# One addition per finished block moves from VectorE to GpSimd, and one pass gets another place in the order list

## The chip, the cores and the metric

The kernel runs on one core of one Trainium2 chip. Its time is the device time of one execution in microseconds (us). Beside it stands one profiled execution, taken by the hardware profiler, whose rows are quoted below: PE is TensorE, DVE is VectorE, ACT is ScalarE, POOL is GpSimd, SP is SyncE, whose only work here is to issue DMA transfers. L1323 is line 1323 of the kernel.

## The reference

One layer mixes 128 context tokens and 2048 latent tokens. Half of the channels go through a recurrence over tokens with a 64 x 64 state for each of 8 heads, once forward and once backward, and the two outputs are added, normalised for each head, gated and sent through an output projection:

```python
def step(S, inp):
    r_t, w_t, k_t, v_t, kk_t, a_t = inp
    s_kk = jnp.einsum('bdhij,bdhj->bdhi', S, kk_t)
    S = (S * w_t[..., None, :] - s_kk[..., :, None] * (kk_t * a_t)[..., None, :]
         + v_t[..., :, None] * k_t[..., None, :])
    return S, jnp.einsum('bdhij,bdhj->bdhi', S, r_t)
...
y = ys[:, 0] + jnp.flip(ys[:, 1], axis=1)
mean = jnp.mean(y, axis=-1, keepdims=True)
var = jnp.mean(jnp.square(y - mean), axis=-1, keepdims=True)
y = ((y - mean) * lax.rsqrt(var + GN_EPS)).reshape(b, t, A_WIDTH)
y = y * lp['gn_w'].astype(f32) + lp['gn_b'].astype(f32)
y = y + (bonus[..., None] * vh).reshape(b, t, A_WIDTH)
...
ya = ya.astype(x.dtype) * jax.nn.silu(g_a)
```

The kernel writes the last three lines as (normalised y) x gn_w x gate + q, where q holds gn_b and the bonus, already multiplied by the gate.

## The kernel before, in words

There are three phases. The first computes all projections and writes what the recurrence needs to HBM. The second is the scan, and the change lies there. The third is the output projection with the last normalisation.

**Stages and bodies of the scan.** The tokens are cut into chunks of 64. A stage handles 8 chunks of one pair of heads in each direction; there are 17 stages. The words of the list `SEQ` are the steps of one body of a software pipeline: `S00+0` is a step for the body's own stage, `zr+2` one for the stage two further on, `L0+4` a load for the stage four further on. Bodies -3 to -1 fill the pipeline, bodies 0 to 12 (up to `FIXED`) are the repeated ones, and after them a second list, `LATE`, gives every step with its stage and mixes in the third phase.

**What sets the order.** From body 0 on, PE, DVE and ACT execute exactly in the order of these lists. POOL and SP don't: their instructions are put in an order by a scheduler that estimates when each is ready. Every engine's queue, SP's too, is served strictly in order.

**The inverse, on POOL.** A chunk needs the inverse of a triangular 64 x 64 matrix. Its diagonal blocks of 32 rows come from step `I`, lines 1091 and 1094: for one stage 15 products (`ztmp`, m = 0 to 14) with two subtractions (`zt`) each, 45 instructions. The step `pre` (L1081, L1082, DVE) comes ahead of it and writes the `ab` that it reads; step `zr` (L1102, DVE) transposes the finished `zt`, after which `U` (L1119, PE) multiplies. In body b, `pre` works for stage b+3 and `zr` for stage b+2, so each inverse lies between the `pre` of one body and the `zr` of the next.

**The end of a block.** Where both directions of a block of 512 tokens are done, seven steps finish it, one block in each body: `fw` fetches the gate `sg` and squares y into `w` (L1298, ACT); `fr` sums the squares; `fq` takes the root (L1303, ACT); `fm` normalises y (L1306, DVE) and fetches q into the one buffer `w`; `T` transposes y into PSUM (L1317, PE); `fy` multiplies by gn_w and the gate (L1321, DVE, from PSUM into `sg`); `fa` adds q (L1323) and issues the store to `mixT` (L1327). `sg` and `w` have one buffer each: the next block's gate is fetched after the store has landed (L1286), and the next squares are written after the addition has read q. There are 17 such ends, 16 of latent blocks and one of the context.

Of the kernel before, what the change touches and what calls it, by code (L numbers as in the profile page):

```python
# [10 lines left out]
ALU = mybir.AluOpType  # L11
# [745 lines left out]
E111 sv71+-1 Ev111 E010 E101 y11+-1 E011 gsL1+2 fsL1+1 bu+1 Ev010 I+2 S20 Ev101 fw Ev011 sv20 S01 E100  # L757
fsL0+1 gsL0+2 sv01 fr Ev100 Gm1+3 Ge1+3 dg1+3 W+1 S11 Qm1+3 gh11+1 gh00+1 ab+3 fq Fm0+3 S30 n+1 Qe1+3 Qm0+3
L0+4 sv11 Fa0+3 Qe0+3 zi+3 sv30 S40 Fe0+3 fm S21 sv40 sv21 Fm1+3 L1+4 X0+1 S50 pre+3 T sv50 Fa1+3 Fe1+3 S31
S60 sv31 Xc00+1 init+1 y00 Xc10+1 X1+1 S41 Xc01+1 sv60 S70 svL0+2 zr+2 sv41 E000+1 sv70 fy Xc11+1 Ev000+1  # L760
zd+2 S51 gh01+2 U+2 y01 Gm0+4 E001+1 c0+2
"""
IN_PM = "E001 E011 E101 E110 Fm1 Gm1 Qm0 Qm1 X1".split()
# [1 line left out]
FIXED = 13  # L765
# [50 lines left out]
def phase2(K):  # L816
    nc, tc, A, S = K.nc, K.tc, K.A, K.S
    V, G, P, T = nc.vector, nc.gpsimd, nc.scalar, nc.tensor
# [99 lines left out]
    def tl(shape, tag, b, pool=None, dt=F32):  # L918
        return (pool or O.l0).tile(shape, dt, tag=tag, name=f"{tag}_{K.u()}", bufs=b)
# [73 lines left out]
    def psum(name, s, shape):  # L993

        pool, tag = pool_of(name, s)
        return pool.tile(shape, F32, tag=tag, name=f"ps{name}_{s}_{K.u()}")
# [253 lines left out]
    def outputs(name, s, st, gi):  # L1250

        g = st.g[gi]
        k = int(name[1])
        u = unit(g, 4 * k + 3)
        m = u % 2 if g.blk is None else u // 4
        ps = g.sp.pop(k)
        p, blk = g.units[0][0], g.blk
        y, there = ynew.setdefault((p, blk), (None, []))
        if y is None:
            y = tl([128, 4, 128], "y", 5)  # L1260
            ynew[p, blk] = y, there
        r = slice(m * 64, m * 64 + 64)
        src = ps[64:128].rearrange("p q h v -> p q (h v)")
        if m in there:
            V.tensor_tensor(y[r], src, y[r], ALU.add)
        else:
            P.copy(y[r], src)
        there.append(m)
        if len(there) == 4:
            ynew.pop((p, blk))  # L1270
            ends[s, gi] = finish(p, blk, y)
            pend.append((s, gi))

    def finish(p, blk, y):

        t0 = NCTX + 512 * blk if blk is not None else 0
        if blk is None:
            parts = [(pp_, slice(pp_ * 128, pp_ * 128 + 128)) for pp_ in range(4)]
        else:
            parts = [(p, slice(0, 512))]  # L1280

        def fetch(nm, t_):
            if blk is None:
                D(t_[:].rearrange("p (g t) -> p g t", t=128), S[nm][:, 0:128].rearrange("(g p) t -> p g t", p=128))
            else:
                D(t_[:], S[nm][p * 128:(p + 1) * 128, t0:t0 + 512])  # L1286

        heads = lambda x: x.rearrange("p q (h v) -> p (q h) v", h=2)
        per_head = lambda x: x[:].unsqueeze(2).broadcast_to((128, 8, 64))
        if blk is None:  # L1290
            mn = tl([128, 8], "ymn", 1)
            V.tensor_reduce(mn[:], heads(y[:]), mybir.AxisListType.X, ALU.add)
            V.scalar_tensor_tensor(heads(y[:]), per_head(mn), -1.0 / 64, heads(y[:]), ALU.mult, ALU.add)
            yield
        sg = tl([128, 512], "sg", 1)
        fetch("sg", sg)
        w = tl([128, 4, 128], "w", 1)
        P.activation(w[:], y[:], AF.Square)  # L1298
        yield
        ss = tl([128, 8], "yss", 2)  # L1300
        V.tensor_reduce(ss[:], heads(w[:]), mybir.AxisListType.X, ALU.add)
        yield
        P.activation(ss[:], ss[:], AF.Sqrt, bias=B.geps[:], scale=1.0 / 64)  # L1303
        yield
        V.reciprocal(ss[:], ss[:])
        V.tensor_tensor(heads(y[:]), heads(y[:]), per_head(ss), ALU.mult)  # L1306
        q = tl([128, 512], "w", 1)
        fetch("q", q)
        yield
        pt = psum("T", 0, [128, 512])  # L1310
        idm = B.idt[:]
        for i in range(4):
            if blk is None:
                dst = pt[:, i * 128:i * 128 + 128]
            else:
                dst = pt[:].rearrange("p (m q t) -> p m q t", m=2, q=4)[:, :, i]
            T.transpose(dst, y[:, i], idm if blk is None else idm.rearrange("p (m t) -> p m t", m=2))  # L1317
        yield
        o = sg
        for g_, cs in parts:  # L1320
            V.scalar_tensor_tensor(o[:, cs], pt[:, cs], B.gwh[:, g_:g_ + 1], sg[:, cs], ALU.mult, ALU.mult)  # L1321
        yield
        V.tensor_tensor(o[:], o[:], q[:], ALU.add)  # L1323
        if blk is None:
            D(S["mixT"][0:512, 0:128].rearrange("(g p) t -> p g t", p=128), o[:].rearrange("p (g t) -> p g t", t=128))
        else:
            D(S["mixT"][p * 128:(p + 1) * 128, t0:t0 + 512], o[:])  # L1327
        K.mixed[blk] = K.mixed.get(blk, 0) + 1
# [4 lines left out]
    def ending(name, s, st, gi):  # L1333
# [3 lines left out]
        if st.fin is not None:  # L1337
# [3 lines left out]
              zr=zrows, zd=zrows, c0=zcopies, c1=zcopies, U=merge, bu=merge, W=merge, n=merge, gh=gcopies, X=solve, Xc=solve,  # L1341
# [307 lines left out]
```

## Time and profile before

| what | us |
|---|---|
| median of three runs (1577.63 to 1589.78) | 1579.01 |
| the profiled execution's own time | 1579.98 |
| its span, first to last instruction | 1578.2 |
| PE busy, of the span | 1496.3 |
| DVE busy | 1138.5 |
| ACT busy | 772.6 |
| POOL busy | 574.6 |
| the 17 inverses on POOL, busy (L1094 217.6 + L1091 138.2) | 355.8 |

The page divides the span into 40 slices of 39.5 us and gives the busy tenths of each engine in each. A group's row gives a line, its engine and operation, the tile it writes and those it reads, its count, and then the busy time, the mean duration in ns and the idle time just before, with what ended it. A row of the timeline gives a start in us from the span's start and a duration. The chain of waits follows the work that ended last back from the end. The repeated bodies that finish a block lie between about 1036 and 1282 us.

### The profile page before, as it was taken

The numbers are of one execution on the slowest core, as the hardware profiler recorded it, in microseconds if no ns is written. First come the engines' busy times: TensorE is split into PE (matmuls) and PEld (weight loads), VectorE is DVE, ScalarE is ACT, GpSimd is POOL, SyncE is SP. The second block draws the span as 40 slices with busy tenths as digits, with TensorE's granted clock in tenths as the row PEclk, the third lists the DMA queues.
The fourth block names the chain that finished last, engine by engine and source line by source line (L and its number), as shares of the span: only waits on it lengthen the run. The fifth ranks groups of instructions, "written<-read, shape, count | busy, mean of one in ns | idle before, by whom it ended". The sixth has DMA issues, their size and how long they took to land.

```text
span 1578.2 us, 39386 instructions
## 1 busy us (share of the span) xinstructions
PE 1496.3 (95%) x16208; PEld 1377.9 (87%) x16208; DVE 1138.5 (72%) x1957; ACT 772.6 (49%) x1462; POOL 574.6 (36%) x962
## 2 busy tenths in 40 slices
PE   5899989999999999999999998999999997799998
PEld 2899989999999999899999997887888786678786
DVE  5999995673999735449995437899898987646533
ACT  4566652432555313225651107887878777523222
POOL 0133320000333100013322805888888887212221
PEclk9999999999999999999999998999999999999999
DMA  9669998663877875447887536566675754645442
GB/s 370 211 186 264 265 266 324 214 217 118 214 228 228 200 241 182 142 140 205 257 252 267 196 124 170 163 185 174 192 202 163 192 157 149 183 139 189 149 143 93
DMA packets 204580, 313.78 MB, mean 199 GB/s; under 512 B 58089, under 2 KB 147561, under 8 KB 190321
## 3 DMA queue, kind: packets, MB, share of 16 engines
q1 hardware_dynamic: 168816, 311.13, 63.6%
q10 hardware_dynamic: 35584, 0.14, 1.4%
q8 instruction: 127, 2.08, 0.6%
q14 instruction: 53, 0.43, 0.1%
HBM read 208.05 MB, written 103.17 MB: 197 GB/s over the span
## 4 chain that ended last, share of the span: by engine, by line
PE 61%; DVE 18%; DMA 8%; issue 5%; POOL 4%; ACT 3%; SPq 1%; ACTq 0%; DVEq 0%; POOLq 0%
PE psu L1503 4%; PE psu L1504 4%; PE psu L1505 4%; PE psE L1189 3%; POOL zt L1094 3%; PE mmb L182 2%; PE mmb L184 2%; PE mmb L183 2%; PE psS L1220 2%; PE mmc L182 2%; PE mmc L184 2%; PE mmc L183 2%; PE mmu L184 2%; PE mmgb L184 2%; PE mmu L182 2%
## 5 line engine op out<-in xcount | busy, mean ns | idle before, releaser
L1094 POOL TENSOR_TENSOR zt<-zt,ztmp 128x30 f32<-128x30 f32 (+7 forms) x510 | 217.6, 427 | 39.8
L1091 POOL TENSOR_TENSOR ztmp<-ab,zt 128x60 f32<-128x60 f32 (+7 forms) x255 | 138.2, 542 | 63.7 <-DVE ab L1082 44.0
L410 POOL TENSOR_TENSOR sh<-rawl 128x384 f32<-128x384 f32 (+1 forms) x48 | 46.9, 994 | 209.9 <-ACT rawl L401 209.9
L1220 PEld LDWEIGHTS psS<-sv,E 128*64 128x64 f32 x2176 | 81.3, 138 | 40.3 <-DVE sv L1246 18.8
L1220 PE MATMUL psS<-sv,E 128*64 128x64 f32 x2176 | 102.2, 229 | 14.8 <-DVE sv L1246 11.0
L1194 DVE TENSOR_TENSOR E<-psE,msk 128x512 f32<-128x512 f32 x136 | 90.6, 683 | 16.6 <-PE psE L1189 15.4
L1568 POOL TENSOR_TENSOR z<-z,x 128x512 f32<-128x512 f32 x32 | 42.7, 1338 | 146.5 <-DVE z L1562 86.0
L1175 ACT ACTIVATE stf<-psX 64x512 f32<-64x512 f32 x136 | 80.3, 591 | 11.2 <-PE psX L1171 8.8
L434 POOL TENSOR_TENSOR hsl<-sq,hsh 128x384 fp32r<-128x384 f32 (+1 forms) x24 | 34.0, 1417 | 130.6 <-ACT hsh L429 130.6
L1246 DVE TENSOR_TENSOR sv<-psS,pc 64x128 f32<-64x128 f32 x254 | 62.7, 273 | 22.5 <-PE psS L1220 21.8
L182 PE MATMUL mmg<-h,w 128*128 128x384 f32 (+1 forms) x216 | 70.8, 328 | 0.0
L183 PE MATMUL mmg<-h,w 128*128 128x384 f32 (+1 forms) x216 | 70.7, 327 | 0.0
L184 PE MATMUL mmg<-h,w 128*128 128x384 f32 (+1 forms) x216 | 70.6, 327 | 0.0
L219 POOL TENSOR_TENSOR hslq<-ssq,hshq 128x384 fp32r<-128x384 f32 (+1 forms) x4 | 4.8, 1208 | 176.9 <-ACT hshq L218 176.9
L182 PE MATMUL mmb<-h,w 128*128 128x384 f32 (+1 forms) x192 | 63.6, 331 | 5.8 <-DMA w<-scr_wsp 3.3
L184 PE MATMUL mmc<-h,w 128*128 128x384 f32 (+1 forms) x192 | 63.5, 331 | 0.9 <-DVE w L154 0.9
L182 PE MATMUL mmv<-h,w 128*128 128x384 f32 (+1 forms) x192 | 63.0, 328 | 1.0 <-DVE sg L524 0.9
L182 PE MATMUL mmc<-h,w 128*128 128x384 f32 (+1 forms) x192 | 63.6, 331 | 0.0
L184 PE MATMUL mmb<-h,w 128*128 128x384 f32 (+1 forms) x192 | 63.5, 331 | 0.0
L183 PE MATMUL mmc<-h,w 128*128 128x384 f32 (+1 forms) x192 | 63.3, 330 | 0.0
L183 PE MATMUL mmb<-h,w 128*128 128x384 f32 (+1 forms) x192 | 63.3, 330 | 0.0
L184 PE MATMUL mmu<-h,w 128*128 128x384 f32 (+1 forms) x192 | 62.8, 327 | 0.0
(312 smaller groups left out, 5009.8 us busy)
## 6 DMA issues: line engine op xcount, KB each, us to landing
w<-scr_wsp SPq DMA_DIRECT2D x68, 1024.0 KB, 6.8
scr_wsp<-w SPq DMA_DIRECT2D x34, 1024.0 KB, 6.1
rr<-scr_ops SPq DMA_DIRECT2D x32, 1024.0 KB, 6.2
scr_ops<-xs SPq DMA_DIRECT2D x160, 192.0 KB, 6.1
wr<-in_win SPq DMA_DIRECT2D x34, 512.0 KB, 6.8
x<-in_x SPq DMA_DIRECT2D x17, 512.0 KB, 3.7
wadas<-in_wada SPq DMA_DIRECT2D x8, 1024.0 KB, 13.7
sv<-scr_vt SPq DMA_DIRECT2D x32, 256.0 KB, 3.8
```

The costliest lines, as they stand in the source:

```text
L182: T.matmul(ps[:, :n], w[:, 0, k], hh[:, 0, k, :n], start=k == 0, stop=False)
L183: T.matmul(ps[:, :n], w[:, 0, k], hh[:, 1, k, :n], start=False, stop=False)
L184: T.matmul(ps[:, :n], w[:, 1, k], hh[:, 0, k, :n], start=False, stop=k == 7)
L1091: G.tensor_tensor(tv, ab[:, j:j + 2, j + 2:32].unsqueeze(1).broadcast_to((128, kn, 2, n)), zt[:, :kn, j:j + 2].unsqueeze(3).broadcast_to(( ...
L1094: G.tensor_tensor(zt[:, :kn, j + 2:32], zt[:, :kn, j + 2:32], tv[:, :, r], ALU.subtract)
L1175: P.activation(g.fs[64:128, :, hd, e::2], g.ps["X"][e][hr_].rearrange("p a (b t) -> p b a t", b=2), AF.Copy, scale=-1.0)
L1194: V.tensor_tensor(g.E[n][:, k:k + 2].rearrange("p a b c -> p (a b) c"), pe[:].rearrange("p a b c -> p (a b) c"), B.msk[:, ME[g.d]].unsquee ...
L1220: T.matmul(g.sp[i // 4][r, q, hd, :], g.E[n][:, k, hd, r], g.sv[:, u, hd, :], start=True, stop=True)
L1246: V.tensor_tensor(dst, g.sp[i // 4][0:64, q], B.pc[0:64, d, 2 * p:2 * p + 2, c:c + 1].broadcast_to((64, 2, 64)), ALU.mult)
L1503: T.matmul(ps[:], mh[:, n], hi[:, cs], start=start and n == 0, stop=False)
L1504: T.matmul(ps[:], mh[:, n], lo[:, cs], start=False, stop=False)
L1505: T.matmul(ps[:], ml[:, n], hi[:, cs], start=False, stop=stop and n == 3)
```

## The change

In the bodies before `FIXED`, the addition of q is issued on GpSimd instead of VectorE; in the work after them it stays on VectorE. The gating pass `fy` moves within the list `SEQ` from behind `sv70` to behind `sv31`, that is from behind `zr` to ahead of it.

```diff
 L0+4 sv11 Fa0+3 Qe0+3 zi+3 sv30 S40 Fe0+3 fm S21 sv40 sv21 Fm1+3 L1+4 X0+1 S50 pre+3 T sv50 Fa1+3 Fe1+3 S31
-S60 sv31 Xc00+1 init+1 y00 Xc10+1 X1+1 S41 Xc01+1 sv60 S70 svL0+2 zr+2 sv41 E000+1 sv70 fy Xc11+1 Ev000+1
+S60 sv31 fy Xc00+1 init+1 y00 Xc10+1 X1+1 S41 Xc01+1 sv60 S70 svL0+2 zr+2 sv41 E000+1 sv70 Xc11+1 Ev000+1
 zd+2 S51 gh01+2 U+2 y01 Gm0+4 E001+1 c0+2
...
         yield
-        V.tensor_tensor(o[:], o[:], q[:], ALU.add)
+        (G if K.body < FIXED else V).tensor_tensor(o[:], o[:], q[:], ALU.add)
         if blk is None:
```

The step `fa` stands third in the list, for the block of the body before (`fa+-1`), and isn't moved there. Since bodies 4 to 12 issue one addition each, 9 of the 17 change engines.

The first place is VectorE at the end of the first body that finishes a block, from the product step `sv31` on. Before, `fy` (L1321) and the addition (L1323) stand behind `zr` (L1102):

```order
L1246 TENSOR_TENSOR sv_10884<-psS_1_0_11467,pc 64x128
L1265 TENSOR_TENSOR y_10355<-psS_0_0_11319,y_10355 64x512
L1246 TENSOR_TENSOR sv_10762<-psS_0_4_11597,pc 64x128
L1102 STREAM_TRANSPOSE zr_11713<-zt_11118 128x32x16
L1246 TENSOR_TENSOR sv_10884<-psS_1_4_11699,pc 64x128
L1321 SCALAR_TENSOR_TENSOR sg_11461<-psT_1238_11657,gwh,sg_11461 128x512
L1194 TENSOR_TENSOR E_1244_11728<-psE_4_1243_11716,msk 128x512
L1105 STREAM_TRANSPOSE zd_11730<-zr_11713 128x512
L1265 TENSOR_TENSOR y_10261<-psS_1_0_11467,y_10261 64x512
L1246 TENSOR_TENSOR sv_10884<-psS_1_4_11699,pc 64x128
L1323 TENSOR_TENSOR sg_11461<-sg_11461,w_11606 128x512
```

The same place on VectorE in the changed kernel:

```order
L1246 TENSOR_TENSOR sv_10884<-psS_1_0_11467,pc 64x128
L1321 SCALAR_TENSOR_TENSOR sg_11461<-psT_1238_11657,gwh,sg_11461 128x512
L1265 TENSOR_TENSOR y_10355<-psS_0_0_11319,y_10355 64x512
L1246 TENSOR_TENSOR sv_10762<-psS_0_4_11597,pc 64x128
L1102 STREAM_TRANSPOSE zr_11714<-zt_11118 128x32x16
L1246 TENSOR_TENSOR sv_10884<-psS_1_4_11700,pc 64x128
L1194 TENSOR_TENSOR E_1244_11728<-psE_4_1243_11717,msk 128x512
L1105 STREAM_TRANSPOSE zd_11730<-zr_11714 128x512
L1265 TENSOR_TENSOR y_10261<-psS_1_0_11467,y_10261 64x512
L1246 TENSOR_TENSOR sv_10884<-psS_1_4_11700,pc 64x128
```

`fy` now stands ahead of `zr`, and the addition is gone from this queue.

The second place is POOL, in the two inverses that take the first two of the moved additions; `zt_11592` is the `zt` of the stage after the one that `zr` transposes above:

```order
@@ -347,4 +347,5 @@
 L1094 TENSOR_TENSOR zt_11592<-zt_11592,ztmp_11892 128x7x18 x2
 L1091 TENSOR_TENSOR ztmp_11892<-ab_11554,zt_11592 128x256
+L1323 TENSOR_TENSOR sg_11461<-sg_11461,w_11606 128x512
 L1094 TENSOR_TENSOR zt_11592<-zt_11592,ztmp_11892 128x8x16 x2
 L1091 TENSOR_TENSOR ztmp_11892<-ab_11554,zt_11592 128x252
@@ -369,4 +370,5 @@
 L1094 TENSOR_TENSOR zt_12074<-zt_12074,ztmp_12378 128x3x26 x2
 L1091 TENSOR_TENSOR ztmp_12378<-ab_12036,zt_12074 128x192
+L1323 TENSOR_TENSOR sg_11943<-sg_11943,w_12088 128x512
 L1094 TENSOR_TENSOR zt_12074<-zt_12074,ztmp_12378 128x4x24 x2
 L1091 TENSOR_TENSOR ztmp_12378<-ab_12036,zt_12074 128x220
```

Every moved addition stands inside an inverse, between a product and its subtractions. Of the nine, those in the first, fourth, fifth and seventh of these inverses stand behind the product of m = 7 (128x256, the middle of the inverse), the other five behind that of m = 3 (128x192).

The third place is SP's queue behind the first of them:

```order
 L1009 DMA rr_8377<-scr_ops_57 128x4x512
 L1009 DMA rr_8378<-scr_ops_59 128x4x512
-L944 DMA sv_11711<-scr_vt 64x8x128
 L1327 DMA scr_mixT<-sg_11461 128x512
 L1286 DMA sg_11943<-scr_sg 128x512
+L944 DMA sv_11712<-scr_vt 64x8x128
 L944 DMA sv_11834<-scr_vt 64x8x128
 L956 DMA stg_9583<-scr_ops_59 64x2x512
```

The store to `mixT`, which waits for the addition, now stands ahead of a load of `sv`, and the loads that follow (`stg`, `stf`, `q` and the next two `rr`) remain behind it.

## The prediction

> **What bounds the kernel now.** I read the page's slices first, for where POOL works at all.
>
> ```profile
> PE   5899989999999999999999998999999997799998
> DVE  5999995673999735449995437899898987646533
> POOL 0133320000333100013322805888888887212221
> ```
>
> POOL is busy in eight tenths from slice 25 to slice 32 (about 990 to 1300 us), the repeated bodies, and hardly elsewhere; PE and DVE are just as full there, so shares of busy time don't say which of the three sets the pace. The groups of 1059.3 to 1282 us do, a stretch that holds nine whole inverses and the nine additions in question. First POOL's groups, all it does in those 222.7 us:
>
> ```profile
> L1094 POOL TENSOR_TENSOR zt<-zt,ztmp 128x78 f32<-128x78 f32 (+4 forms) x270 | 117.3, 434 | 21.2
> L1091 POOL TENSOR_TENSOR ztmp<-ab,zt 128x60 f32<-128x60 f32 (+4 forms) x136 | 73.9, 543 | 10.6
> ```
>
> Busy 117.3 + 73.9 and idle 21.2 + 10.6 make 223.0, the whole stretch. The idle time has no releaser: it is the gap of 31.8 / 406 = 0.08 us ahead of each instruction. POOL never waits for work here. Now who waits for POOL, among the groups of DVE in the same stretch:
>
> ```profile
> L1102 DVE STREAM_TRANSPOSE zr<-zt 128x512 f32<-128x512 f32 x10 | 10.7, 1074 | 7.7 <-POOL zt L1094 7.6
> ...
> L1321 DVE SCALAR_TENSOR_TENSOR sg<-psT,gwh,sg 128x512 f32<-128x512 f32 x9 | 6.5, 724 | 0.0
> ...
> L1323 DVE TENSOR_TENSOR sg<-sg,w 128x512 f32<-128x512 f32 x9 | 6.0, 672 | 0.0
> ```
>
> DVE, whose queue is in order, stands still for 7.6 us in all until an inverse is done, and the addition itself waits for nothing. One turn of the loop in the timeline, POOL first and then DVE and PE:
>
> ```profile
> 1083.43 0.60 POOL L1094 TENSOR_TENSOR zt<-zt,ztmp 128x30 f32<-128x30 f32 x2
> 1084.11 0.29 POOL L1091 TENSOR_TENSOR ztmp<-ab,zt 128x60 f32<-128x60 f32 x1
> ```
>
> ```profile
> 1059.64 1.06 DVE L1102 STREAM_TRANSPOSE zr<-zt 128x512 f32<-128x512 f32 x1
> ...
> 1080.81 0.69 DVE L1082 TENSOR_TENSOR ab<-ab,dg 128x512 f32<-128x512 f32 x1
> ...
> 1082.28 0.47 DVE L1246 TENSOR_TENSOR sv<-psS,pc 64x128 f32<-64x128 f32 x2
> 1084.07 1.08 DVE L1102 STREAM_TRANSPOSE zr<-zt 128x512 f32<-128x512 f32 x1 [1.31 <-POOL zt L1094]
> ```
>
> ```profile
> 1080.68 0.66 PE L1317 MATMUL psT<-idt,y 128*128 128x128 f32 x4
> ...
> 1083.95 1.05 PE L1189 MATMUL psE<-sth,stf 128*64 128x128 f32 x16
> ...
> 1086.24 1.07 PE L1119 MATMUL psU<-zr,GA 32*32 32x32 f32 x57 [0.48 <-DVE sg L1321]
> ...
> 1088.36 0.89 PE L1019 MATMUL psGm<-rr 64*64 64x128 f32 x24
> ```
>
> An inverse ends at 1084.03, `zr` starts 0.04 later, and the next inverse starts at 1084.11 on an `ab` that was ready at 1081.50, 2.61 us earlier. A body takes 1084.07 - 1059.64 = 24.4 us, and that is what 45 instructions take on POOL. So POOL sets the period of these bodies, with DVE a close second (its wait ahead of `zr` is 0 to 1.7 us).
>
> **The change, part by part.** *What POOL gains in work.* Nine additions of 128x512, one in each of the inverses that nine `zr` wait for. POOL does the same shape later, in the third phase:
>
> ```profile
> L1568 POOL TENSOR_TENSOR z<-z,x 128x512 f32<-128x512 f32 x32 | 42.7, 1338 | 146.5 <-DVE z L1562 86.0 <-DVE z L1560 40.1 <-DMA mxa<-scr_mixT 12.7
> ```
>
> Its mean of 1.34 us and the gap of 0.08 make 1.42 an inverse.
>
> *What POOL gets back.* While the addition ran on DVE, POOL was slower. The same two subtractions of 128x96, first undisturbed, then in two bodies where L1323 ran beside them, and below them DVE's row for the first of those:
>
> ```profile
> 967.38 0.85 POOL L1094 TENSOR_TENSOR zt<-zt,ztmp 128x96 f32<-128x96 f32 x2
> ...
> 1063.50 1.54 POOL L1094 TENSOR_TENSOR zt<-zt,ztmp 128x96 f32<-128x96 f32 x2
> ...
> 1162.53 1.19 POOL L1094 TENSOR_TENSOR zt<-zt,ztmp 128x96 f32<-128x96 f32 x2
> ```
>
> ```profile
> 1063.64 0.67 DVE L1323 TENSOR_TENSOR sg<-sg,w 128x512 f32<-128x512 f32 x1
> ```
>
> The excess is 0.69 in one and 0.34 in the other. I take the middle, 0.52, since both kinds occur. Net, an inverse grows by 1.42 - 0.52 = 0.90 us (ends 0.73 and 1.08), and nine by 8.1 (6.6 to 9.7). On POOL's clock that is not hidden by anything: there is no idle time to fill.
>
> [...]
>
> *What DVE is spared.* 0.67 us a body for the addition, and the 0.72 of `fy` leaves the place behind `zr` for one ahead of it. At 1082.28 to 1082.75 the two `sv` steps end and DVE idles until 1084.07, and `fy`'s input from PE is complete at 1081.34, so there it fits into the wait. None of this shortens a body while POOL sets the period, with one exception: behind the last of these `zr` no further moved addition follows. There the chain of waits reads
>
> ```profile
> 1283.30 0.66 DVE sg L1321
> 1283.96 0.14 issue
> 1284.09 1.30 PE psU L1119 x62
> ```
>
> PE's `U` needs a PSUM buffer that `fy` frees, which is already free in the new order. I take 0.7 off the sum once (0 to 1.4, both savings). The work behind starts from that `U` and is otherwise shifted whole. Over the whole span, the answer on L1102 reads
>
> ```profile
> its engine sat idle before it (us, times) until:
>   POOL zt L1094: 7.6, 6
> ```
>
> and all of those 7.6 us lie in the stretch, so the inverses after it have room.
>
> *What is queued behind the late addition.* It now ends late in four of the nine inverses, those where it stands behind m = 7:
>
> ```profile
> 1070.30 0.63 POOL L1091 TENSOR_TENSOR ztmp<-ab,zt 128x256 f32<-128x256 f32 x1
> ```
>
> The product ends at 1070.93, or 1070.4 without the excess; the addition would end at 1071.8 instead of 1064.31. ACT must not overwrite `w` earlier:
>
> ```profile
> 1067.75 0.63 ACT L1298 ACTIVATE w<-y 128x512 f32<-128x512 f32 x1
> ...
> 1072.88 0.30 ACT L1303 ACTIVATE yss<-yss,geps 128x8 f32<-128x8 f32 x1 [2.20 <-DVE yss L1301]
> 1074.50 1.19 ACT L1130 ACTIVATE zb<-psW 32x512 f32<-32x512 f32 x2 [1.32 <-PE psW L1127]
> ```
>
> L1298 slips by 4.1 us; the idle 2.20 + 1.32 ahead of the next two groups takes up 3.5, and the 0.6 that is left is less than the 2.61 by which `ab` is early. So I cost it at nothing. On SP the store waits as long, and behind it the loads:
>
> ```profile
> 1064.34 0.33 SPq L1327 DMA_DIRECT2D scr_mixT<-sg  x1
> 1066.37 0.33 SPq L1286 DMA_DIRECT2D sg<-scr_sg  x1
> ...
> 1071.13 1.77 SPq L956 DMA_DIRECT2D stf<-scr_ops  x2
> ...
> 1073.65 1.13 SPq L1286 DMA_DIRECT2D w<-scr_q  x1
> 1077.45 2.50 SPq L1009 DMA_DIRECT2D rr<-scr_ops  x2
> ```
>
> ```profile
> rr<-scr_ops SPq DMA_DIRECT2D x16, 1024.0 KB, 5.6
> ...
> stf<-scr_ops SPq DMA_DIRECT2D x18, 256.0 KB, 5.1
> ```
>
> With the store at 1071.8 the gate's fetch goes at 1073.8, and some seven issues of about 0.6 us (from the row of two `stf` in at most 1.77) put `stf` near 1076 and `rr` near 1079, 5 and 1.5 us late. `rr` lands 5.6 later, near 1084.6, ahead of its use at 1088.36; `stf` lands near 1081 to 1083, by an estimate from these rows, ahead of the next stage's operators at 1083.95. Hidden too, with little room. In the other five the addition stands near where it stood, and nothing waits longer.
>
> *The sum:* 8.1 - 0.7 = +7.4 us on the profiled execution's 1579.98 (span 1578.2 and 1.8 around it), which stands 1.0 above the median of 1579.01. On the median: **1586.4 us**. With the ends of the terms, 6.6 - 1.4 to 9.7: 1584.2 to 1588.7.
>
> **The rivals.** A measurement of this kernel can tell about 1% from no change, 15.8 us: below 1563.2 or above 1594.8.
>
> *POOL gets nothing back.* If the lengthening of its pairs returns elsewhere in the inverse (other additions on DVE then meet it), each inverse costs the full 1.42: 12.8 - 0.7 = +12.1, 1591. [...] For it: the excess varies between bodies. Against it: 0.69 beside a DVE instruction of 0.67.
>
> *The waits behind the late addition decide.* If in the four inverses the 4.1 us of ACT or the 5 us of `stf` are not absorbed, `ab` or the operators come late; then the loop is no longer POOL's. What exceeds the 2.61 of room is 1.5 to 2.4 us each if one of them lies wholly on the path, and up to 4.1 each without that room: +6 to +16 on top, 1592 to 1603. It decides from the point where a body behind PE and DVE takes longer than POOL's by more than `ab` is early. For it: the four bodies whose `zr` does not wait are nearly even.
>
> *The other side: DVE is the limit and POOL only looks full.* Its place is the stretch of each body around `zr`; it decides if POOL's additions cost less than the 0.52 or so that POOL recovers plus what DVE's shorter queue brings forward. Then nine bodies lose the addition's 0.67, and at most `fy`'s 0.72 too: -6.0 to -12.5, 1566.5 to 1573. For it: six of the ten `zr` wait for POOL, and the other four do not. Against it: 223.0 of 222.7 us are POOL's, and it is given more.
>
> *Nothing moves.* The added work ends in room that I don't see, such as a different meeting of POOL with the other DVE additions: 1579, give or take 2. That the change doesn't do what it says is excluded by the order: nine additions stand on POOL.
>
> **How the numbers follow.** Forecast 0.62, nothing back 0.14, waits 0.11, DVE the limit 0.06, nothing moves 0.07. The forecast's own range of 1584 to 1589 is widened by the rivals: from 1579, which takes in half of the no-change case, to 1595, which takes in the first rival and the lower part of the waits; outside lie some 0.17. Slower by over 1% needs three quarters of the waits' span: 0.08. Faster by over 1% is beyond even the far end of the third: 0.02. Within 1%: 0.90.
>
> **What would show it.** In the changed profile L1323 should appear nine times on POOL with a mean near 1.3 us; the pair of 128x96 should fall to 0.85; an inverse should take about 0.9 longer; the wait of `zr` for POOL should grow from 7.6 us, to 10 or more, and the idle time of POOL stay without a releaser. ACT should wait for POOL ahead of L1298 in four bodies. I am wrong if POOL is seen to wait for `ab` (L1082), if `zr` no longer waits, or if L1568's duration doesn't hold in the middle of an inverse.

## The result and the profile after

The changed kernel's median over 20 runs is 1591.82 us (1585.75 to 1600.53), that of the kernel before, over 20 runs beside it, 1582.04 (1577.63 to 1592.88). The ratio is 1.0055 with a 95% interval of 1.004 to 1.007, that is +8.7 us (6.3 to 11.1) on 1580. Two later comparisons beside the experiments gave 1.0071 (1.0054 to 1.0088) and 1.0075 (1.0046 to 1.0103). The change costs 9 to 12 us, within 1%.

The profiled execution took 1596.18 us (span 1594.4). It is 16.2 above the profiled one of before and so shows more than the medians do. About 3 us of that need not be the change's: the body behind the last of the nine inverses, from one `zr` to the next, took 31.6 us in the profile of before and 34.9 in this one, but 34.8 and 36.7 in those of two kernels below that cost nothing (fy_only and store_ctl). Over the nine bodies themselves, from the `zr` at 1059.6 to the one at 1281.9 before and from 1061.4 to 1294.9 after, the change took 233.5 instead of 222.3 us.

The page's slices of the changed kernel, PE and POOL:

```profile
PE   5899999999999999999999988998989997899998
POOL 0133330001333100013314606888878786212221
```

Counted from 0, as in the prediction, PE has eights in slices 23, 24, 27 and 29 (before only in 24), and POOL's row of eights from slice 25 on is broken by sevens in 29 and 31. The groups of 1060.4 to 1294.7 us, which hold the nine moved additions, POOL first and then DVE:

```profile
L1094 POOL TENSOR_TENSOR zt<-zt,ztmp 128x78 f32<-128x78 f32 (+4 forms) x270 | 109.0, 404 | 20.4
L1091 POOL TENSOR_TENSOR ztmp<-ab,zt 128x60 f32<-128x60 f32 (+4 forms) x135 | 72.1, 534 | 21.2 <-DVE ab L1082 11.0
L1323 POOL TENSOR_TENSOR sg<-sg,w 128x512 f32<-128x512 f32 x9 | 11.4, 1269 | 0.7 <-DMA w<-scr_q 0.7
...
L1037 DVE TENSOR_TENSOR GA<-psGm,mkg 128x512 f32<-128x512 f32 x36 | 23.1, 684 | 15.6 <-PE psGm L1019 15.1
L1102 DVE STREAM_TRANSPOSE zr<-zt 128x512 f32<-128x512 f32 x9 | 9.5, 1055 | 0.9 <-POOL zt L1094 0.9
```

The wait for `psGm` before, in 1059.3 to 1282 us:

```profile
L1037 DVE TENSOR_TENSOR GA<-psGm,mkg 128x512 f32<-128x512 f32 x36 | 23.1, 681 | 3.1 <-PE psGm L1019 2.7
```

The nine additions stand on POOL at 1.27 us each. But POOL, which never waited for work before, now waits 11.0 us for `ab`, and `zr` waits for POOL 0.9 us instead of 7.6. POOL no longer sets the pace everywhere. Its busy time has hardly grown: 109.0 + 72.1 + 11.4 = 192.5 us against 117.3 + 73.9 = 191.2 before. The new wait is DVE's for `psGm`, 15.1 us instead of 2.7.

The waits of 1059 to 1296 us name what stands behind it:

```profile
engine line waited for: us in total, times, longest us
DVE GA L1037 <- PE psGm L1019: 15.1, 6, 4.6
ACT w L1298 <- POOL sg L1323: 12.0, 3, 4.4
POOL ztmp L1091 <- DVE ab L1082: 11.0, 4, 3.8
...
PEld psGm L1019 <- DMA rr<-scr_ops: 4.4, 2, 3.7
...
PEld psE L1189 <- DMA stf<-scr_ops: 3.3, 2, 3.1
```

PE waits for loads, `rr` and `stf`. SP's queue in the timeline behind the first late addition (POOL's addition ends at 1072.56):

```profile
1072.59 0.33 SPq L1327 DMA_DIRECT2D scr_mixT<-sg  x1
1076.97 0.33 SPq L1286 DMA_DIRECT2D sg<-scr_sg  x1
1077.41 1.27 SPq L944 DMA_DIRECT2D sv<-scr_vt  x2
1078.77 0.58 SPq L956 DMA_DIRECT2D stg<-scr_ops  x1
1079.41 1.59 SPq L956 DMA_DIRECT2D stf<-scr_ops  x2
1081.05 0.60 SPq L956 DMA_DIRECT2D stg<-scr_ops  x1
1081.70 0.59 SPq L1286 DMA_DIRECT2D w<-scr_q  x1
1082.39 1.12 SPq L1009 DMA_DIRECT2D rr<-scr_ops  x2
```

Before, the issues from the gate's fetch to `rr` were spread over 11.1 us (1066.37 to 1077.45 in the prediction's rows), with some 2.5 us of nothing ahead of `stg` and ahead of `rr`. Now the store waits for the addition, the gate's fetch for the store, and the loads leave back to back within 5.4 us. The chain of waits goes through the first of the two `rr`:

```profile
1082.39 10.61 DMA rr<-scr_ops
...
1093.04 1.98 PE psGm L1019 x32
...
1103.21 1.04 PE psGm L1019 x32
```

It takes 10.61 us to land; the group of all `rr` of the stretch says the same (KB each, median us to landing), first before and then after:

```profile
rr<-scr_ops SPq DMA_DIRECT2D x16, 1024.0 KB, 5.6
```

```profile
rr<-scr_ops SPq DMA_DIRECT2D x16, 1024.0 KB, 8.7
```

And the 32 matmuls that wait for it take 1.98 us, where the same 32 take 1.04 ten microseconds later. That is the granted clock. Three stretches of 4 us in that body (busy time of PE, PEld, DVE, ACT and POOL, then clock, DMA share, GB/s):

```profile
1084.00:1088.00 4.00, 1.83 (x48) 1.42 (x46) 2.26 (x6) 3.89 (x8) 3.14 (x12) 1.00 1.08 202
1088.00:1092.00 4.00, 3.29 (x76) 3.18 (x78) 1.48 (x3) 1.31 (x3) 3.05 (x6) 0.66 1.04 368
1092.00:1096.00 4.00, 3.44 (x60) 2.97 (x58) 0.94 (x2) 3.56 (x7) 3.37 (x9) 0.50 0.91 285
```

The share of the DMA engines is 0.91 to 1.12 while the loads land (1080 to 1096), PE is busy for only 1.83 of the 4 us from 1084 on, and then has a clock of 0.66 and 0.50. While the store waited, the same share was 0.01 to 0.20 (1064 to 1076 us).

### The profile page after: what moved, and what is told of

The parts are those of the page before. It is cut to its first block, busy times and chain, and to the rows that moved or that the text cites. A ratio compares the mean times of both kernels' runs of the same rounds, so it can differ in the third digit from the quotient of the medians.

```text
span 1594.4 us, 39381 instructions
## 1 busy us (share of the span) xinstructions
PE 1504.9 (94%) x16208; PEld 1386.4 (87%) x16208; DVE 1136.4 (71%) x1948; ACT 772.2 (48%) x1462; POOL 569.6 (36%) x971
## 4 chain that ended last, share of the span: by engine, by line
PE 64%; DVE 16%; DMA 10%; issue 5%; ACT 2%; SPq 1%; ACTq 0%; POOL 0%; DVEq 0%
PE psE L1189 5%; PE psu L1503 4%; PE psu L1504 4%; PE psu L1505 4%; PE psS L1220 3%; PE psGm L1019 2%; DMA rr<-scr_ops 2%; PE mmb L182 2%; PE mmb L184 2%; PE mmb L183 2%; DVE E L1194 2%; DVE ab L1063 2%; PE mmu L182 2%; PE mmu L184 2%; PE mmgb L184 2%
## 5 line engine op out<-in xcount | busy, mean ns | idle before, releaser
L1094 POOL TENSOR_TENSOR zt<-zt,ztmp 128x30 f32<-128x30 f32 (+7 forms) x510 | 206.2, 404 | 39.1
L1568 POOL TENSOR_TENSOR z<-z,x 128x512 f32<-128x512 f32 x32 | 42.7, 1338 | 149.1 <-DVE z L1562 86.3
L1037 DVE TENSOR_TENSOR GA<-psGm,mkg 128x512 f32<-128x512 f32 x68 | 43.6, 684 | 30.8 <-PE psGm L1019 30.4
L184 PE MATMUL mmc<-h,w 128*128 128x384 f32 (+1 forms) x192 | 62.8, 327 | 1.0 <-DVE w L154 1.0
L182 PE MATMUL mmc<-h,w 128*128 128x384 f32 (+1 forms) x192 | 63.0, 328 | 0.0
## 6 DMA issues: line engine op xcount, KB each, us to landing
wadas<-in_wada SPq DMA_DIRECT2D x8, 1024.0 KB, 13.9
```

The costliest lines, as they stand in the source:

```text
L182: T.matmul(ps[:, :n], w[:, 0, k], hh[:, 0, k, :n], start=k == 0, stop=False)
L184: T.matmul(ps[:, :n], w[:, 1, k], hh[:, 0, k, :n], start=False, stop=k == 7)
L1094: G.tensor_tensor(zt[:, :kn, j + 2:32], zt[:, :kn, j + 2:32], tv[:, :, r], ALU.subtract)
```

## The experiments

Two theories were on trial. The first is the forecast's: POOL's added work lengthens each inverse, and that is the loss. The second is the rival that took the waits behind the late addition as decisive, with two suspects, SP's queue behind the store and ACT's wait for `w`. All results, each against runs of the kernel before on the same chip:

| run | median us | before us | ratio | 95% interval |
|---|---|---|---|---|
| fy_only | 1579.24 | 1579.18 | 1.0001 | 0.9984 to 1.0017 |
| add_only | 1607.8 | 1579.18 | 1.0181 | 1.0151 to 1.021 |
| early | 1585.43 | 1579.18 | 1.0038 | 1.0023 to 1.0053 |
| early_again | 1584.46 | 1577.78 | 1.0038 | 1.002 to 1.0056 |
| unblocked | 1594.88 | 1579.18 | 1.0095 | 1.0069 to 1.0121 |
| store_ctl | 1577.95 | 1576.63 | 0.9999 | 0.9985 to 1.0014 |
| store_late | 1583.89 | 1576.63 | 1.0046 | 1.0028 to 1.0064 |
| store_mid | 1579.72 | 1578.08 | 1.001 | 0.9995 to 1.0026 |
| late_w | 1579.16 | 1576.63 | 1.0012 | 0.9998 to 1.0025 |
| rebuilt | 1594.43 | 1578.08 | 1.0082 | 1.0052 to 1.0111 |
| after_again | 1588.88 | 1576.63 | 1.0071 | 1.0054 to 1.0088 |
| after_third | 1588.92 | 1577.78 | 1.0075 | 1.0046 to 1.0103 |

Losses in us below are the ratio's excess times 1580, with the ratio as the comparison gave it, which isn't the quotient of the two medians.

### The two halves of the change: fy_only and add_only

fy_only keeps the move in the list and leaves the addition on VectorE:

```diff
-        (G if K.body < FIXED else V).tensor_tensor(o[:], o[:], q[:], ALU.add)
+        V.tensor_tensor(o[:], o[:], q[:], ALU.add)
```

> The move in the list alone: fy (L1321) stands ahead of zr, the addition stays on VectorE. POOL's and SP's order are those of before. Both theories: 0 to -3 us, a ratio of 0.998 to 1.000. If instead the earlier fy delays zr and so the path, +2 to +6 us, and the loss of the change would partly be that of the move.

Measured 0.2 us (-2.5 to +2.7). The move of `fy` is worth nothing that can be measured.

add_only is the other half; `fy` stays behind `sv70`:

```diff
-S60 sv31 fy Xc00+1 init+1 y00 Xc10+1 X1+1 S41 Xc01+1 sv60 S70 svL0+2 zr+2 sv41 E000+1 sv70 Xc11+1 Ev000+1
+S60 sv31 Xc00+1 init+1 y00 Xc10+1 X1+1 S41 Xc01+1 sv60 S70 svL0+2 zr+2 sv41 E000+1 sv70 fy Xc11+1 Ev000+1
```

> The other half alone: the addition is on POOL, fy keeps its old place behind zr. The additions then stand still later in their inverses, behind m = 9 to 11 in four of them and behind m = 5 in five. If POOL's extra work makes the loss, it is that of the changed kernel, +7 to +8 us, a ratio of 1.005. If the waits behind the late addition make it, it is larger, +12 to +20 us, a ratio of 1.008 to 1.013.

Measured +28.6 us (24 to 33), more than expected even by the second theory. POOL's work is the same as in the changed kernel, so lateness can cost 17 to 20 us more than the change does. Its waits in the repeated bodies:

```profile
ACT w L1298 <- POOL sg L1323: 31.3, 4, 9.5
POOL ztmp L1091 <- DVE ab L1082: 28.2, 7, 5.4
DVE yss L1301 <- ACT w L1298: 15.9, 4, 5.8
```

Here ACT waits 7.8 us in the mean of the four bodies, and DVE's sum of squares (L1301), which has to be executed in its place in the queue, waits for ACT. PE then waits 13.1 us, in four waits of up to 5.1, for what DVE makes behind it (`GA`, L1037). In the changed kernel ACT waits 12.0 us in these bodies, in three of the four, and L1301 2.1 us in the whole run. The store is as much later as the addition here, so how the 28.6 us divide between ACT's wait and SP's queue is not shown. The move of `fy`, worth nothing by itself, keeps the moved addition out of this.

### POOL's work without the lateness: early and early_again

In the bodies POOL too executes in the order of the list, which puts each addition ahead of an inverse instead of in its middle. Work and SP's order are those of the changed kernel. The store goes even earlier than before the change, 0.4 to 1.2 us behind a body's `zr` instead of 4.0 to 4.9.

```diff
-        order = tc.manual_schedule(engines={mybir.EngineType.PE, mybir.EngineType.DVE, mybir.EngineType.Activation})
+        three = {mybir.EngineType.PE, mybir.EngineType.DVE, mybir.EngineType.Activation}; order = tc.manual_schedule(engines=three | {mybir.EngineType.Pool})
...
-        K.body = FIXED
+        K.body = FIXED; order.__exit__(None, None, None); order = tc.manual_schedule(engines=three); order.__enter__()
```

> As the changed kernel, but in the bodies POOL too executes in the order of the list, so that each of the nine additions stands ahead of an inverse instead of in its middle. The work of POOL is that of the changed kernel; the addition ends about where it ended on VectorE, so neither ACT nor SP waits longer than before the change. If POOL's extra work makes the loss (0.8 to 0.9 us in each of nine inverses), it stays at +6 to +8 us against the kernel before, a ratio of 1.004 to 1.005, and the wait of zr (L1102) for POOL grows beyond the 7.6 us of before. If the waits behind the late addition make it, it goes down to 0 to +2 us, a ratio of 1.000 to 1.001, and the waits for psGm (L1037 on VectorE) fall back from 30.8 to about 13 us.

> The changed kernel with the nine additions ahead of the inverses once more, beside the changed kernel itself. If the late additions cost something beyond POOL's work, it stays at +5 to +7 us, a ratio of 1.003 to 1.0045, and 3 to 5 us under the run beside it. If POOL's work is all there is, the two agree within 1.5 us.

Measured 1.0038 both times, +6.0 us (3.6 to 8.4 and 3.2 to 8.8). The first theory's mechanism is there: POOL is full, as the forecast said. POOL's groups in 1063 to 1291.2 us, and the waits of `zr` in that stretch:

```profile
L1094 POOL TENSOR_TENSOR zt<-zt,ztmp 128x78 f32<-128x78 f32 (+4 forms) x270 | 111.9, 415 | 21.2
L1091 POOL TENSOR_TENSOR ztmp<-ab,zt 128x60 f32<-128x60 f32 (+4 forms) x136 | 75.0, 551 | 10.0
L1323 POOL TENSOR_TENSOR sg<-sg,w 128x512 f32<-128x512 f32 x9 | 11.5, 1276 | 0.6 <-DVE sg L1321 0.6
...
L1102 DVE STREAM_TRANSPOSE zr<-zt 128x512 f32<-128x512 f32 x10 | 10.8, 1078 | 11.7 <-POOL zt L1094 11.6
```

POOL's busy and idle time make 230.2 in 228.2 us: it is full, and `zr` waits 11.6 us for it, 4.0 more than before. The nine bodies, from the `zr` at 1063.4 to the one at 1291.0, take 227.6 us instead of 222.3, that is 5.3 more, or 0.6 a body. An addition between two inverses, in POOL's timeline:

```profile
1087.21 0.61 POOL L1094 TENSOR_TENSOR zt<-zt,ztmp 128x30 f32<-128x30 f32 x2
1087.77 1.28 POOL L1323 TENSOR_TENSOR sg<-sg,w 128x512 f32<-128x512 f32 x1
1089.00 0.29 POOL L1091 TENSOR_TENSOR ztmp<-ab,zt 128x60 f32<-128x60 f32 x1
```

The addition starts just before the subtractions ahead of it end (1087.82), and the next product just before the addition ends, so the two inverses stand 1.18 us apart instead of 0.08. It costs 1.1 us and has no gap of its own.

Against the changed kernel beside it (1588.92, 1.0075) early_again is 4.5 us faster by the medians, 6.4 by the means, give or take 4. With the other two measurements of the change, the late additions cost some 3 to 6 us beyond POOL's work.

### A store further back: unblocked

The addition keeps its place on POOL; the store becomes a step of its own behind `gsL0+2`, the gate's fetch moves from `fw` to `fr`, and SP executes in the order of the list.

```diff
-fsL0+1 gsL0+2 sv01 fr Ev100 Gm1+3 Ge1+3 dg1+3 W+1 S11 Qm1+3 gh11+1 gh00+1 ab+3 fq Fm0+3 S30 n+1 Qe1+3 Qm0+3
+fsL0+1 gsL0+2 fz+-1 sv01 fr Ev100 Gm1+3 Ge1+3 dg1+3 W+1 S11 Qm1+3 gh11+1 gh00+1 ab+3 fq Fm0+3 S30 n+1 Qe1+3 Qm0+3
...
-        sg = tl([128, 512], "sg", 1)
-        fetch("sg", sg)
+        early = K.body >= FIXED
+        sg = early and tl([128, 512], "sg", 1)
+        early and fetch("sg", sg)
         w = tl([128, 4, 128], "w", 1)
         P.activation(w[:], y[:], AF.Square)
         yield
+        sg = sg or tl([128, 512], "sg", 1)
+        early or fetch("sg", sg)
```

> As the changed kernel, with the additions in the same places among POOL's instructions, but the store of the finished block is a step of its own further back in the list, the gate's fetch comes after it, and SP executes in the order of the list in these bodies, so that the loads of sv, stg, stf and rr of a body no longer stand behind a store that waits for a late addition. ACT's L1298 still waits for the addition. If POOL's extra work makes the loss, nothing changes: +6 to +9 us, a ratio of 1.004 to 1.006. If SP's queue behind the late addition makes it, it falls to 0 to +3 us, a ratio of 1.000 to 1.002, and the wait for psGm falls back towards 13 us. If it is ACT's wait, it stays at +6 to +9 while the wait for psGm goes.

It missed: +15.0 us (10.9 to 19.1), worse than the change. The timeline of SP in one of its bodies shows why:

```profile
1182.55 0.54 SPq L1331 DMA_DIRECT2D scr_mixT<-sg  x1
1189.16 0.33 SPq L1286 DMA_DIRECT2D sg<-scr_sg  x1
1189.58 0.39 SPq L1009 DMA_DIRECT2D rr<-scr_ops  x1
```

`stg` and `stf` did go ahead of the store, but the gate's fetch waits 6.6 us for the store to land, and `rr` stands behind the fetch. The edit moved the wait from loads with room to the load with the least. It separates nothing cleanly; it shows that holding up SP's queue at another place can cost more than the change does.

### The store's lateness alone: store_ctl, store_late, store_mid

All three leave the nine additions on VectorE in their old place, with POOL's order as before. store_ctl makes the store a step of its own, `fz`, with the loads behind it in the list, and lets SP execute in that order, which in the nine bodies is SP's order of before. store_late holds the store back in the four bodies in question:

```diff
         V.tensor_tensor(o[:], o[:], q[:], ALU.add)
         yield from [0] * (K.body < FIXED)
+        if K.body in (4, 7, 8, 10):
+            V.tensor_copy(o[:, 0:8], o[:, 0:8])
```

store_mid is store_late with the step `fz` earlier in the list, behind `Ev110` instead of behind `Ev011`.

> Control for the next one: the kernel before, all nine additions on VectorE in their old place, but SP executes in the order of the list in the bodies, with the store as a step of its own and the loads of sv, stg and stf behind it, which is the order that SP has before. Expected 0 +- 2 us against the kernel before, a ratio of 0.999 to 1.001.

> As that control, and in the four bodies whose addition stands behind m = 7 in the changed kernel VectorE copies 8 columns of the finished sg onto themselves about 8 us after the addition, so that the store waits for it, and the gate's fetch and the loads behind it on SP wait too. POOL has no work more than before, and w is free as early as before. If SP's queue behind a late store is what the late additions cost, +8 to +14 us against the control, with waits of PE for rr or stf in these four bodies. If POOL's work is the only cost, 0 to +1 (four copies of about 0.1 us).

> As the run with the late store, with the copy that holds the store placed half as late: the store goes about 4 us later than in the control instead of 8, so that the loads behind it end about when rr is issued in the control. If a late store costs only what it takes beyond the room ahead of rr's issue, 0 to +2 us against the control and rr lands in 5.5 to 7 us. If every us by which the store is late costs, about half of +7.5, +3 to +5.

How late the store goes in the four bodies is read from SP's timelines, in one profile of each kernel, behind the body's `zr`:

| run | us from `zr` to store | later than in its reference |
|---|---|---|
| before | 4.7, 4.9, 4.7, 4.0 | |
| changed kernel | 11.1, 11.6, 12.1, 10.5 | 6.4, 6.7, 7.4, 6.5 |
| store_ctl | 4.7, 4.9, 4.7, 4.0 | 0 |
| store_mid | 8.9, 9.4, 9.6, 8.4 | 4.2, 4.5, 4.9, 4.3 |
| store_late | 12.4, 12.9, 16.6, 12.4 | 7.7, 8.0, 11.9, 8.4 |

The control measured -0.2 us (-2.4 to +2.2). With the store about 8 us late, and 12 in one body, it is +7.3 (4.4 to 10.1), just below what was expected; with 4 to 5 us, +1.6 (-0.8 to +4.1). POOL's instructions are the same in all three, and a pass of VectorE over 128x8 takes 0.16 to 0.20 us in the profile of before (L286 to L288, L1305), so the four copies make less than 1 us. So a late store is enough to cost as much as POOL's additions do. The change's store is later than store_mid's and earlier than store_late's, and one load of `sv` more stands behind it. So what its lateness costs was not measured alone; it should lie between 1.6 and 7.3 us if the cost grows with the lateness. That the cost begins at a threshold is suggested, not shown: if every microsecond cost the same, store_mid would cost 3.6, which its interval holds, but in its profile PE waits for no load. The landing of `rr` in the repeated bodies, in store_ctl, store_mid and store_late:

```profile
rr<-scr_ops SPq DMA_DIRECT2D x16, 1024.0 KB, 5.4
```

```profile
rr<-scr_ops SPq DMA_DIRECT2D x16, 1024.0 KB, 7.6
```

```profile
rr<-scr_ops SPq DMA_DIRECT2D x16, 1024.0 KB, 9.5
```

The timelines of SP in the first of the four bodies, for `rr`, in the same order:

```profile
1072.07 2.51 SPq L1009 DMA_DIRECT2D rr<-scr_ops  x2
```

```profile
1072.96 2.46 SPq L1009 DMA_DIRECT2D rr<-scr_ops  x2
```

```profile
1075.91 0.97 SPq L1009 DMA_DIRECT2D rr<-scr_ops  x2
```

The `zr` ahead of them start at 1054.20, 1055.06 and 1055.30, so `rr` is issued 17.9, 17.9 and 20.6 us after it. In store_mid it leaves on time and takes 2.2 us longer to land, with the other loads leaving just ahead of it (5.5 to 7 us were expected, 7.6 were measured); in store_late it leaves 2.7 late and takes 4.1 longer besides.

### ACT's wait alone: late_w

Additions and stores in their old places; in the same four bodies VectorE reads 8 columns of `w` late, in a step of its own behind `Ev011`, so that ACT can't overwrite it.

```diff
             D(S["mixT"][p * 128:(p + 1) * 128, t0:t0 + 512], o[:])
+        if K.body in (4, 7, 8, 10):
+            yield
+            V.tensor_copy(tl([128, 8], "dum", 1)[:], q[:, 0:8])
```

> The kernel before, additions and stores in their old places; in the same four bodies VectorE copies 8 columns of w to a scratch tile about 8 us after the addition, so that ACT's L1298, which overwrites w, waits about 4 us as in the changed kernel, and nothing else does. If the wait of ACT is hidden by its idle time ahead of L1303 and L1130, 0 to +1 us. If it is what the late additions cost, +8 to +14 us.

```profile
ACT w L1298 <- DVE dum L1331: 15.5, 4, 4.8
```

ACT waits 3.9 us in the mean of the four (4.5, 4.8, 4.3 and 2.0), about as in the changed kernel (3.5, 4.0 and 4.5 in three of them), and the whole costs +1.9 us (-0.3 to +4.0): not told from nothing. ACT's wait is mostly hidden, as the prediction had it; a cost of up to 4 us is not excluded.

### The parts put together: rebuilt

early and store_late in one kernel, with `fy` in its new place.

> The two causes that were each measured alone, put together: POOL adds q in the nine bodies ahead of its inverse (alone +6.0 us), fy stands in its new place, and in the four bodies a copy of 8 columns by VectorE holds the store back (alone about +7.5). ACT does not wait for w. If the two causes lie in the same bodies and hide one another, it costs what the changed kernel costs, +8.5 to +11.5 us, a ratio of 1.0055 to 1.0075, and in the four late bodies zr no longer waits for POOL. If they add up, +13 to +14 us, a ratio of 1.0085.

Measured +13.0 us (8.2 to 17.5). It suits the sum of the two parts, 13.4, better than the change's 9 to 12, but the interval holds both. The combination is no copy of the change: in the third of the four bodies its store goes 16.0 us behind `zr`, 4 later than the change's, and it has a wait of its own. What its additions waited for:

```profile
its engine sat idle before it (us, times) until:
  DMA w<-scr_q: 5.1, 2
```

The late queue of SP also brings q late, and an addition that stands ahead of the inverse then holds up the whole inverse. In the changed kernel the addition stands in the inverse's middle and waited 0.7 us for q. Whether the two causes add up or partly hide one another in the change stays open.

### The changed kernel again: after_again, after_third

> The changed kernel unchanged, beside the next three, so that its loss (+8.7 us at first) stands against the same runs of before and its trace can be read a second time. Expected +6 to +11 us, a ratio of 1.004 to 1.007, and waits for late rr or stf again in the bodies of the additions behind m = 7 only.

> The changed kernel beside the next run, on the same chip, to settle how much of its loss is left without the late additions. So far +8.7 and +11.2 us; expected +8 to +12, a ratio of 1.005 to 1.0075.

Measured +11.2 (8.5 to 13.9) and +11.8 us (7.3 to 16.3). In these profiles too PE stands still for 1 to 3 us in the bodies with a late addition or right behind one, for `rr` or `stf` where the profile names what it waited for, and `zr` waits for POOL in two or three of the nine only. The profiles differ in how much of POOL's time is waiting for `ab`: 3.8 and 5.8 us here, 11.0 in the first.

No version here is faster than the kernel before; fy_only, store_ctl, store_mid and late_w can't be told from it.

## Why the prediction was right or wrong

**The time.** 1586.4 was forecast from a median of 1579.01, +7.4; measured is 1591.82, which lies in the range, and +8.7 in the comparison that gave it. The two later comparisons say 11 to 12, above the +5.2 to +9.7 of the forecast's own range and inside the whole one. The class, within 1%, is right. That +7.4 comes so near +8.7 is partly luck: the term for POOL was too large and the loads behind the store were put at nothing, and the two errors have opposite signs.

**What POOL gains and gets back: right in kind, too large in size.** The addition takes 1.27 us, predicted 1.34 from L1568. The subtractions fall from 434 to 415 ns in early and the products rise from 543 to 551, over 30 and 15 of them: 0.57 - 0.12 = 0.45 us returned an inverse, predicted 0.52. In the inverse that holds the first late addition the pair of 128x96 is undisturbed:

```profile
1064.64 0.86 POOL L1094 TENSOR_TENSOR zt<-zt,ztmp 128x96 f32<-128x96 f32 x2
```

It was 1.54 with DVE's addition beside it. So the rival in which POOL gets nothing back is out. In the nine bodies of before, the POOL instruction that met DVE's addition took longer every time: by 0.34 to 0.52 us in the five in which DVE's addition started first, and by 0.68 to 0.71 in the four in which POOL's did. So both kinds occur, as the prediction took it from two bodies, and its 0.52 lies between them.

But the sum of 1.27 + 0.08 - 0.45 = 0.90 an inverse isn't what a body takes. The gap of 0.08 that was added isn't there: the addition moves the next product by 1.1 us, less 0.45 that makes some 0.65, and the nine bodies of early show 5.3 us, 0.6 each, where 8.1 were reckoned. early's +6.0 agrees with that; its interval holds 8.1 too.

In the changed kernel POOL gets back more: the busy time of its products and subtractions falls by 191.2 - 181.1 = 10.1 us against 191.2 - 186.9 = 4.3 in early. It falls most in three of the nine inverses, to 18.9 to 19.0 us, where the other six take 20.5 to 20.9. DVE stands still for 3.4 to 6.2 us during those three, but for 7.9 during one of the six, so why it falls is not shown.

**POOL sets the period: right before the change, and no longer in most bodies after it.** The prediction named the sign by which it would be wrong, POOL waiting for `ab`: it waits 11.0 us, and `zr` waits 0.9, in two bodies, where 10 or more were to be seen. In five of the nine an inverse is finished 1.7 to 6.3 us ahead of its `zr`. The forecast's picture is that of early, not of the changed kernel.

**What is queued behind the late addition: the step that failed.** ACT's half held: L1298 waits 4 us in three of these bodies, and late_w shows such a wait costing nothing that can be told. SP's half, "Hidden too, with little room", did not. Three sizes in it were low. Between store and gate's fetch 2.0 us were assumed, and it took 4.4. `rr` was to go 1.5 us late; it goes 20.9 us after the body's `zr` (1082.39 - 1061.45) instead of 17.8 (1077.45 - 1059.64), 3.1 late, and the first `stf` 18.0 instead of 11.5, 6.5 late where 5 were reckoned. Above all its landing was taken over from before, 5.6 us, and it took 10.61. The duration of a transfer was treated as a property of the transfer, while seven others were moved to just ahead of it. So the room of 3.8 us that the prediction worked out for `rr` (1084.6 to 1088.36) met 1.6 + 5.0 us more than it reckoned with.

**The rival of the waits.** It had the right place, the bodies around the four late additions, and the right sign, `zr` that no longer waits for POOL, and priced it at 6 to 16 us on top. early against the change says 3 to 6. So it is smaller than its price, and no alternative to the forecast: POOL's work costs without it (early) and it costs without POOL's work (store_late). How the 9 to 12 us of the change divide between the two is open. In its first profile the nine bodies grew by 11.2 us while POOL's busy time grew by 1.3 and POOL waited 11.0 for `ab`; in the two later profiles they grew by 6.7 and 8.4, with 3.8 and 5.8 of waiting for `ab`.

**What DVE is spared: not seen.** The 0.7 us taken off for `fy` can't be told from nothing in fy_only. That `fy` had to move for another reason, to bring the addition forward, shows in add_only: left in its old place it would have made the loss 17 to 20 us larger.

**DVE is the limit, and nothing moves:** both out, by the sign of every comparison.

## What to carry to other kernels

Before an operation is given to an engine with a later place for it, follow its result into the queues of the other engines, the one that issues the transfers above all: here a store that waited held up the loads behind it (the first `stf` by 6.5 us, `rr` by 3.1), and the loads that then left together took longer to land (`rr` 8.7 us in the median instead of 5.6), so the landing time of the spread-out case may not be taken over. Find how much lateness the cover takes: in four bodies, 4 to 5 us on the store cost 1.6 us in all and about 4 on `w` cost 1.9, neither to be told from nothing, and 8 to 12 us on the store cost 7.3. And take the price of an added operation from the distance between its neighbours, not from its duration and a gap: 1.1 us here instead of 1.35.

## What the runs showed of the hardware

**Behind some of its waits PE ran at a lower granted clock.** In 1055 to 1296 us the granted clock was 1.00 before and 0.96 in the changed kernel (columns as in the stretches above), first before and then after:

```profile
1055.00:1296.00 241.00, 224.73 (x5788) 197.68 (x5780) 220.41 (x446) 189.89 (x362) 206.73 (x438) 1.00 0.66 184
```

```profile
1055.00:1296.00 241.00, 220.34 (x5458) 194.83 (x5460) 207.09 (x418) 179.10 (x344) 197.66 (x427) 0.96 0.65 177
```

The two later profiles of the changed kernel show 0.97 there, those of the kernels that can't be told from before 0.98 to 0.99. 0.04 of 241 us is 9.6 us of full clock not granted, an upper bound for what it cost against this profile of before, since not all of PE's work is on the path; against the others it is a quarter to three quarters of that. In the changed kernel the pieces of low clock in these bodies lie behind waits of PE. PE's timeline of the changed kernel, at the first and the second late addition:

```profile
1088.71 1.28 PE L1189 MATMUL psE<-sth,stf 128*64 128x128 f32 x13 [2.87 <-DMA stf<-scr_ops]
...
1169.53 1.99 PE L1019 MATMUL psGm<-rr 64*64 64x128 f32 x32 [3.60 <-DMA rr<-scr_ops]
1171.44 1.97 PE L1189 MATMUL psE<-stf,stg 128*64 128x128 f32 x16
```

Two groups of the same lines, shapes and counts before, behind a wait of 0.80 us:

```profile
1088.36 1.10 PE L1019 MATMUL psGm<-rr 64*64 64x128 f32 x32
1089.39 1.09 PE L1189 MATMUL psE<-stf,sth 128*64 128x128 f32 x16
```

So 3.60 us of waiting were followed by 1.8 us of slower matmuls in these two groups alone. The clock was 0.50 in 1168 to 1172, 0.68 in 1172 to 1176 and 1.00 in the 4 us after that. Behind the wait of 2.87 us it was 0.66 in 1088 to 1092, 0.50 in 1092 to 1096 and 0.99 in 1096 to 1100, and behind two waits of 1.96 us, which end at 1221.75 and 1246.10, it was 0.78 to 0.80 over 8 us. Not every wait had this behind it: one of 1.22 us, which ends at 1189.08, is followed by a clock of 1.00 up to 1196. In store_mid the clock was 0.57 in 1084 to 1088, behind 4 us in which PE had stood still for 1.5 in all.

**The loads issued back to back landed later, though none of them was larger.** `rr`, 1024 KB in every run, took 5.4 to 5.7 us in the median with the loads spread out (store_ctl, before, early), and 7.6, 8.7 and 9.5 as they bunched (store_mid, the changed kernel, store_late), with the DMA engines' share at 1.12, 1.08, 1.04 and 0.91 in the four stretches of 4 us from 1080 to 1096 of the changed kernel.
